# A row-sum kernel: the one-element copy ahead of the last VectorE operation becomes a waiting no-op, and SyncE's wait for ScalarE gets a no-op of its own

## The chip, the cores and the metric

One core of one Trainium2 chip; the experiments were spread over three chips, each beside the kernel before. The metric is device time in microseconds (us) of one execution. The profiler records one execution of each kernel; its span is some 1.8 us shorter than the device time. Nanoseconds (ns) below are the trace's own marks.

## The reference

```python
def setup_inputs():
    return {"x": np.random.randn(32, 512, 1024).astype(np.float32)}

def reference(x):
    return np.sum(x, axis=-1).astype(np.float32)
```

16,384 rows of 1,024 fp32 numbers are each summed: 67 MB in, 64 KB out.

## The kernel before

Rows go over the 128 partitions in two blocks of 112 and 16 rows a partition, 16 rows to a load. VectorE sums nearly all of them behind the loads. ScalarE helps towards the end. The change lies in the last block's last rows:

```python
CUT = 544
...
    part = rpool.tile([P, 1], F32, name="part")
    seen = rpool.tile([P, 1], F32, name="seen")
...
    def pairs_dve(xt, a, b, first, acc, pairs):
        h = (a + b) // 2
        nc.vector.tensor_tensor_reduce(
            out=pairs[:, 0 : h - a], in0=xt[:, a:h], in1=xt[:, h:b], scale=1.0, scalar=first,
            op0=ADD, op1=ADD, accum_out=acc,
        )
...
    cuts = [0, 9, 13, 15]            # loads of rows 0-8, 9-12, 13-14 ...
    last = 15 * D
    for i, k in ((0, CUT), (CUT, D)):    # ... and row 15 in two pieces
        nc.sync.dma_start(out=xt[:, last + i : last + k], in_=...)
...
    pairs_dve(xt, 13 * D, 14 * D, 0.0, res[:, c + 13 : c + 14], pairs[2])
    rows_act(xt, res, 14, 1, c + 14)
    pairs_dve(xt, last, last + CUT, 0.0, part, pairs[0])
    nc.vector.tensor_copy(out=seen, in_=part)
    pairs_dve(xt, last + CUT, last + D, part, res[:, c + 15 : c + 16], pairs[1])
    nc.sync.dma_start(out=out_b, in_=res)
```

One such operation adds the columns in pairs and sums the results, from `first` on. In the trace it is two instructions on the engine, the operation and a read of the accumulator (441 and 84 ns for row 15's first piece). Row 15's first piece leaves its sum in `part` (the *carried sum*), and the second piece starts from there. The copy to `seen` is of no use as a copy: it waits for `part` on a semaphore (a counter; the trace has it counted up at 157.703 us, 12 ns after the accumulator read's end, and the copy starts 23 ns later), and the operation behind it starts after the copy does: 99 ns after it.

Of the kernel before, what the change touches and what calls it, by code (L numbers as in the profile page):

```python
# [1 line left out]

# [4 lines left out]

F32 = mybir.dt.float32
ADD = mybir.AluOpType.add
COPY = mybir.ActivationFunctionType.Copy  # L10
X = mybir.AxisListType.X

BLOCKS = (112, 16)
G = 16
ACT_ROWS = 7
CUT = 544
EARLY = 2


@with_exitstack  # L20
def row_sums(
    ctx: ExitStack,
    tc: tile.TileContext,
    x: bass.AP,
    out: bass.AP,
):
    nc = tc.nc
    P = nc.NUM_PARTITIONS

    x_flat = x.flatten_outer_dims()  # L30
    R, D = x_flat.shape
    C = R // P
    assert R % P == 0 and sum(BLOCKS) == C
    out_flat = out.rearrange("a (b c) -> (a b c)", c=1)

    xpool = ctx.enter_context(tc.tile_pool(name="x", bufs=3))
    rpool = ctx.enter_context(tc.tile_pool(name="res", bufs=1))
    part = rpool.tile([P, 1], F32, name="part")
    seen = rpool.tile([P, 1], F32, name="seen")
    pairs = [rpool.tile([P, D // 2], F32, name=f"pairs{i}") for i in range(3)]  # L40

    def rows_dve(xt, res, j, n, c):
        nc.vector.tensor_reduce(  # L43
            out=res[:, c : c + n],
            in_=xt[:, j * D : (j + n) * D].rearrange("p (j d) -> p j d", d=D),
            axis=X,
            op=ADD,
        )

    def sum_act(v, acc):  # L50
        nc.scalar.activation(out=v, in_=v, func=COPY, accum_out=acc)  # L51

    def rows_act(xt, res, j, n, c):
        for i in range(n):
            sum_act(xt[:, (j + i) * D : (j + i + 1) * D], res[:, c + i : c + i + 1])

    def pairs_dve(xt, a, b, first, acc, pairs):
        h = (a + b) // 2
        nc.vector.tensor_tensor_reduce(  # L59
            out=pairs[:, 0 : h - a], in0=xt[:, a:h], in1=xt[:, h:b], scale=1.0, scalar=first,  # L60
            op0=ADD, op1=ADD, accum_out=acc,
        )

    def block(r0, n):
        x_b = x_flat[r0 : r0 + P * n].rearrange("(p c) d -> p (c d)", p=P)
        out_b = out_flat[r0 : r0 + P * n].rearrange("(p c) -> p c", p=P)
        return x_b, out_b, rpool.tile([P, n], F32, name=f"res{r0}")

    full = C - G
    done = 0  # L70
    for b, n in enumerate(BLOCKS):
        x_b, out_b, res = block(done * P, n)
        final = b == len(BLOCKS) - 1
        whole = n - G if final else n
        c = 0
        while c < whole:
            m = min(G, whole - c)
            xt = xpool.tile([P, G * D], F32, tag="xt", name="xt")
            parts = (0, 1, m) if done + c == 0 else (0, m)
            for i, k in zip(parts, parts[1:]):  # L80
                nc.sync.dma_start(
                    out=xt[:, i * D : k * D], in_=x_b[:, (c + i) * D : (c + k) * D]
                )
            a = ACT_ROWS if done + c + m == full else 0
            rows_dve(xt, res, 0, m - a, c)
            rows_act(xt, res, m - a, a, c + m - a)
            c += m
        if not final:

            for i, k in ((0, 104), (104, P)):  # L90
                nc.scalar.dma_start(out=out_b[i:k], in_=res[i:k])
        done += n

    xt = xpool.tile([P, G * D], F32, tag="xt", name="xt")
    cuts = [0, 9, 13, 15]
    for i, k in zip(cuts, cuts[1:]):
        nc.sync.dma_start(out=xt[:, i * D : k * D], in_=x_b[:, (c + i) * D : (c + k) * D])  # L97
    last = 15 * D
    for i, k in ((0, CUT), (CUT, D)):
        nc.sync.dma_start(  # L100
            out=xt[:, last + i : last + k],
            in_=x_b[:, c * D + last + i : c * D + last + k],
        )

    for i, k in zip(cuts[:2], cuts[1:3]):
        h = (k - i) // 2
        rows_dve(xt, res, i, h, c + i)
        rows_act(xt, res, i + h, k - i - h, c + i + h)
    pairs_dve(xt, 13 * D, 14 * D, 0.0, res[:, c + 13 : c + 14], pairs[2])
    rows_act(xt, res, 14, 1, c + 14)  # L110
    pairs_dve(xt, last, last + CUT, 0.0, part, pairs[0])


    nc.vector.tensor_copy(out=seen, in_=part)  # L114
    pairs_dve(xt, last + CUT, last + D, part, res[:, c + 15 : c + 16], pairs[1])
    nc.sync.dma_start(out=out_b, in_=res)


def kernel(tc: tile.TileContext, x: bass.AP, out: bass.AP):
    row_sums(tc, x, out)  # L120
    tc.close()
    tc.compile()  # L122



    sp = mybir.EngineType.SP
    fn = tc.nc.m.functions[0]
    entry, body = None, None
    for blk in fn.blocks:
        ops = [i for i in blk.instructions if i.engine == sp]  # L130
        if entry is None:
            entry = blk
        elif any(i.opcode == "DMACopy" for i in ops):
            body = blk
            break
    code = list(body.instructions)
    loads = [i for i in code if i.engine == sp][:EARLY]
    for load in loads:
        assert load.opcode == "DMACopy" and not load.sync_info.on_wait
        code.remove(load)  # L140
    body.instructions = code
    code = list(entry.instructions)
    at = next(k for k, i in enumerate(code) if i.engine == sp and i.opcode == "Drain")
    code[at:at] = loads
    entry.instructions = code

# [1 line left out]
_INS = ['x']  # L148
_OUTS = [((32, 512), 'float32')]


# [23 lines left out]
```

## Time and profile before

| | |
|---|---|
| device time, median of 6 runs beside the changed kernel (of 3 at the time of the prediction: 162.18 us) | 162.02 us (161.98 to 162.34) |
| span of the profiled run | 160.6 us |
| loads and their queue | 97.2% of the 16 engines' span |
| VectorE busy | 121.4 us, 76% |
| last piece's arrival to the store's issue | 563 ns |
| end of the first accumulator read to the store's issue | 673 ns |

The first rows say that the stream of loads sets the time; the last two are the stretch that the change can touch. The lines of that stretch stand in the prediction. One more view, the chain of waits followed back from the end, is worth having (start and duration in us; "issue" is time for which the profile shows no reason):

```profile
157.68 0.02 DVE part L59
157.70 0.02 issue
157.73 0.15 DVE seen L114
157.88 0.41 DVE pairs L59
```

It makes the copy (`seen`) a link of 0.15 us. It can't show that the last operation had begun at 157.82, before that link's end.

### The profile page before, as it was taken

What the parts mean: (1) busy time and instruction counts of PE and PEld (TensorE: products, weight loads), DVE (VectorE), ACT (ScalarE), POOL (GpSimd) and SP (SyncE); (2) the same over time, 40 slices, a digit from 0 to 9 for tenths busy, and PEclk for the clock granted to TensorE, in tenths of its full rate; (3) what the DMA queues carried; (4) which work ended last, traced back from release to release, by engine and by line L of the source; (5) the groups of instructions that cost most, each with busy time, mean ns of one, the idle gap of its engine ahead of it and who ended that gap; (6) DMA issues with size and microseconds to landing.
All of it is one profiled execution on the core that took longest, in us unless ns stands there. A gap on an engine that the chain in (4) does not pass through costs nothing.

```text
span 160.6 us, 120 instructions
## 1 busy us (share of the span) xinstructions
DVE 121.4 (76%) x16; ACT 17.2 (11%) x31; POOL 0.2 (0%) x4
## 2 busy tenths in 40 slices
DVE  0000059997799958999499994999949999598884
ACT  0000000000000000000000000000000000596892
POOL 0000000000000000000000000000000000000000
DMA  9997996996996996996996979979969969998991
GB/s 375 490 398 337 490 522 294 490 522 261 522 506 278 522 506 278 522 506 278 522 506 278 522 326 457 522 310 473 522 294 490 522 261 522 432 432 369 410 402 62
DMA packets 2169, 67.18 MB, mean 418 GB/s; under 512 B 505, under 2 KB 633, under 8 KB 889
## 3 DMA queue, kind: packets, MB, share of 16 engines
q1 hardware_dynamic: 2016, 67.12, 97.2%
q10 hardware_dynamic: 153, 0.06, 0.1%
HBM read 67.11 MB, written 0.07 MB: 418 GB/s over the span
## 4 chain that ended last, share of the span: by engine, by line
DMA 75%; DVE 22%; SPq 0%; issue 0%; DVEq 0%
DMA xt<-in_x_dram 75%; DVE res L43 21%; DVE pairs L59 1%; SPq L97 0%; DVE seen L114 0%; DVE part L59 0%; DVEq L122 0%; DVE res L59 0%
## 5 line engine op out<-in xcount | busy, mean ns | idle before, releaser
L43 DVE TENSOR_REDUCE res<-xt 128x16 f32<-128x16384 f32 (+3 forms) x9 | 119.8, 13309 | 36.6 <-DMA xt<-in_x_dram 36.6
L51 ACT ACT_TABLE_LOAD x1 | 1.3, 1283 | 138.3 <-DMA xt<-in_x_dram 138.3
L51 ACT ACTIVATE xt<-xt 128x1024 f32<-128x1024 f32 x15 | 15.6, 1042 | 2.2 <-DMA xt<-in_x_dram 2.2
L51 ACT ACTIVATION_READ_ACCUMULATOR xt<-xt 128x1 f32 x15 | 2.8, 186 | 0.0
L59 DVE CUSTOM_DVE_ANT_0 pairs<-xt 128x512 f32<-128x512 f32 (+1 forms) x2 | 1.1, 566 | 0.3 <-DMA xt<-in_x_dram 0.3
L59 DVE CUSTOM_DVE_ANT_0 pairs<-xt,part 128x240 f32<-128x240 f32 x1 | 0.5, 467 | 0.0
L114 DVE COPY seen<-part 128x1 f32<-128x1 f32 x1 | 0.2, 153 | 0.0
L59 DVE DVE_READ_ACCUMULATOR2_ANT res<- 128x1 f32 x2 | 0.2, 81 | 0.0
L159 POOL MEMSET const-bfloat16-1.0<- 128x1 bf16 x1 | 0.1, 101 | 0.0
L159 POOL MEMSET const-uint8-127<- 128x1 uint8 x1 | 0.1, 101 | 0.0
L159 POOL MEMSET const-float32-0.0<- 128x1 f32 x1 | 0.1, 98 | 0.2 <-issue 0.2
L159 POOL MEMSET const-float32-1.0<- 128x1 f32 x1 | 0.1, 98 | 0.0
L59 DVE DVE_READ_ACCUMULATOR2_ANT part<- 128x1 f32 x1 | 0.1, 84 | 0.0
## 6 DMA issues: line engine op xcount, KB each, us to landing
xt<-in_x_dram SPq DMA_DIRECT2D x1, 7680.0 KB
xt<-in_x_dram SPq DMA_DIRECT2D x1, 4608.0 KB, 32.4
xt<-in_x_dram SPq DMA_DIRECT2D x1, 2048.0 KB, 36.9
xt<-in_x_dram SPq DMA_DIRECT2D x1, 1024.0 KB, 39.0
xt<-in_x_dram SPq DMA_DIRECT2D x1, 512.0 KB, 3.9
xt<-in_x_dram SPq DMA_DIRECT2D x1, 272.0 KB, 39.1
xt<-in_x_dram SPq DMA_DIRECT2D x1, 240.0 KB, 38.9
xt<-in_x_dram SPq DMA_DIRECT2D x6, 40.9
```

Of the source, the lines that this page charges most:

```text
L43: nc.vector.tensor_reduce(out=res[:, c : c + n], in_=xt[:, j * D : (j + n) * D].rearrange("p (j d) -> p j d", d=D), axis=X, op=ADD,)
L51: nc.scalar.activation(out=v, in_=v, func=COPY, accum_out=acc)
L59: nc.vector.tensor_tensor_reduce(out=pairs[:, 0 : h - a], in0=xt[:, a:h], in1=xt[:, h:b], scale=1.0, scalar=first, op0=ADD, op1=ADD, accum ...
L114: nc.vector.tensor_copy(out=seen, in_=part)
L159: nc = _bacc.Bacc("TRN2", target_bir_lowering=False, num_devices=1)
```

## The change

The intent: take the copy's time off the end by waiting in an instruction that does nothing else, and let the last store wait for VectorE directly.

```diff
-CUT = 544
+CUT = 576
...
-    pairs_dve(xt, last, last + CUT, 0.0, part, pairs[0])
-    nc.vector.tensor_copy(out=seen, in_=part)
-    pairs_dve(xt, last + CUT, last + D, part, res[:, c + 15 : c + 16], pairs[1])
-    nc.sync.dma_start(out=out_b, in_=res)
+    carry = pairs_dve(xt, last, last + CUT, 0.0, part, pairs[0])
+    tc.keep_in_program_order(nc.vector.keepalive_nop([nc.vector.lower_ap(part)]))
+    total = pairs_dve(xt, last + CUT, last + D, part, res[:, c + 15 : c + 16], pairs[1])
+    tc.declare_no_dep(total.ins, carry.ins, reason="the wait is in the nop before it")
+    tc.keep_in_program_order(nc.sync.keepalive_nop([nc.sync.lower_ap(res[:, c + 14 : c + 15])]))
+    store = nc.sync.dma_start(out=out_b, in_=res)
+    for i in by_act:
+        tc.declare_no_dep(store.ins, i.ins, reason="the wait is in the nop before it")
```

(The tile `seen` goes, and the helpers return their instructions; `by_act` holds ScalarE's of the last block.) `keepalive_nop` is the no-op: it waits until the named tile is written and, in the trace, counts up a semaphore of its own when the wait is over (VectorE's no-op after the change: the carried sum's semaphore comes at 157.425 us, the no-op lasts from 157.452 to 157.473). `declare_no_dep` keeps the scheduler from adding a wait of its own.

More of the change, by code (lines that the diff above doesn't have):

```diff
@@ L38, in row_sums @@
     part = rpool.tile([P, 1], F32, name="part")
-    seen = rpool.tile([P, 1], F32, name="seen")
     pairs = [rpool.tile([P, D // 2], F32, name=f"pairs{i}") for i in range(3)]
@@ L50, in sum_act @@
     def sum_act(v, acc):
-        nc.scalar.activation(out=v, in_=v, func=COPY, accum_out=acc)
+        return nc.scalar.activation(out=v, in_=v, func=COPY, accum_out=acc)
+    by_act = []
     def rows_act(xt, res, j, n, c):
         for i in range(n):
-            sum_act(xt[:, (j + i) * D : (j + i + 1) * D], res[:, c + i : c + i + 1])
+            by_act.append(
+                sum_act(xt[:, (j + i) * D : (j + i + 1) * D], res[:, c + i : c + i + 1])
+            )
     def pairs_dve(xt, a, b, first, acc, pairs):
         h = (a + b) // 2
-        nc.vector.tensor_tensor_reduce(
+        return nc.vector.tensor_tensor_reduce(
             out=pairs[:, 0 : h - a], in0=xt[:, a:h], in1=xt[:, h:b], scale=1.0, scalar=first,
@@ L103, in row_sums @@
         )
+    by_act.clear()
     for i, k in zip(cuts[:2], cuts[1:3]):
```

## The prediction

> **What bounds the kernel now.** I read the page's split of the ending chain first, to see what the 160.6 us span is made of.
>
> ```profile
> DMA 75%; DVE 22%; SPq 0%; issue 0%; DVEq 0%
> HBM read 67.11 MB, written 0.07 MB: 418 GB/s over the span
> ```
>
> The kernel streams 67.11 MB and is bound by that stream nearly everywhere: 67.11 MB / 418 GB/s = 160.6 us. VectorE's 22% of the chain are reductions after which a load buffer comes free. The change touches nothing in there: it alters only what VectorE and SyncE do for the last row of the last block. So the whole question lies after about 156.6 us, and I read the timeline there: start, duration (both us), engine, line, operation, idle time before it.
>
> ```profile
> 156.62 0.69 DVE L59 CUSTOM_DVE_ANT_0 pairs<-xt 128x512 f32<-128x512 f32 x1 [0.26 <-DMA xt<-in_x_dram]
> 157.24 0.08 DVE L59 DVE_READ_ACCUMULATOR2_ANT res<- 128x1 f32 x1
> 157.24 0.44 DVE L59 CUSTOM_DVE_ANT_0 pairs<-xt 128x272 f32<-128x272 f32 x1
> 157.61 0.08 DVE L59 DVE_READ_ACCUMULATOR2_ANT part<- 128x1 f32 x1
> 157.73 0.15 DVE L114 COPY seen<-part 128x1 f32<-128x1 f32 x1
> 157.82 0.47 DVE L59 CUSTOM_DVE_ANT_0 pairs<-xt,part 128x240 f32<-128x240 f32 x1
> 158.22 0.08 DVE L59 DVE_READ_ACCUMULATOR2_ANT res<- 128x1 f32 x1
> 158.36 0.35 SPq L116 DMA_DIRECT2D out_dram<-res  x1
> ```
>
> The copy to be removed is the fifth line. The next operation starts at 157.82, before the copy's end at 157.88. It seems to be released by the copy, and the chain of waits counts the copy as a link. But the last 480 columns also have to be there. The issues of the last two loads and the time from issue to landing say when:
>
> ```profile
> 118.12 0.44 SPq L100 DMA_DIRECT2D xt<-in_x_dram  x1
> 118.91 0.33 SPq L100 DMA_DIRECT2D xt<-in_x_dram  x1
> DMA to landing us min/median/max: 38.9/39.0/39.1
> ```
>
> 118.12 + 39.1 = 157.22 for the first piece (544 columns) and 118.91 + 38.9 = 157.81 for the second. (To the nanosecond the trace's arrivals are 157.217 and 157.801; the last operation starts at 157.825, 24 ns after its data.) That 24 ns is what every operation here needs when data release it: row 13's load lands at 156.601 and the operation starts at 156.625. So **the last operation is released by its data, with the copy at most level with it.** This is the reading on which the prediction rests.
>
> [...] Directly released: 24 ns from landing to start, as above. Behind a wait of its own there is one case on VectorE, at the first reduction, whose data are complete at 21.977 us by the trace's arrivals:
>
> ```profile
> L43 DVEq EVENT_SEMAPHORE  x1: 21/21/21, 22.0 to 22.0; - x1
> 22.08 17.22 DVE L43 TENSOR_REDUCE res<-xt 128x16 f32<-128x16384 f32 x1 [22.08 <-DMA xt<-in_x_dram]
> ```
>
> 22.076 - 21.977 = 99 ns instead of 24 ns. [...] The trace has the sizes: from 272 to 512 columns the time grows by 692 - 441 = 251 ns, 1.046 ns a column, so 157 ns of either is fixed, and the copy's 153 ns is nothing else. The one with the carried scalar is 467 - 251 = 216: 59 ns more than the rule. Either it waits inside for the copy (0.41 us from the copy's end to its own end is just 251 + 157), or fetching a scalar from SBUF costs that much.
>
> **The change, part by part.**
>
> *CUT 544 to 576.* The pairs go from 272 and 240 to 288 and 224 columns. No byte more is moved, so the last landing stays at 157.80. The first piece is 32 columns x 4 B x 128 = 16 KB longer and lands 16 KB / 418 GB/s = 39 ns later, at 157.256; its operation starts at about 157.280 instead of 157.243 and takes 458 instead of 441 ns, so the carried sum is there (with its accumulator read, 7 ns behind the operation's end, and 12 ns for the semaphore) at about 157.757 instead of 157.703. The last operation is 16 columns, 17 ns, shorter.
>
> *The copy goes, a wait comes.* By the 99 ns above, the last operation can start at 157.757 + 0.099 = 157.856. Its data let it start at 157.825. So the wait ends last, and the start moves **31 ns later** although a 153 ns instruction is gone. The duration is 467 - 17 = 450 if the scalar fetch is what costs 59 ns, 391 if the copy did it. End: 158.306 or 158.247, against 158.292 before: **+14 or -45 ns**. I give two chances in three to the fetch, since the 272-column operation likewise began before its forerunner's end (157.243 against 157.317) and paid nothing for it: 14 x 2/3 - 45 x 1/3 = -6 ns.
>
> *SyncE's wait for ScalarE moves ahead.* In the kernel before, the built program has the wait on VectorE's result in an instruction of its own, and the store behind it carries the wait on ScalarE, long fulfilled. The accumulator read ends at 158.300, that wait ends at 138.27 + 20.07 = 158.33, the store is issued at 158.364: 64 ns.
>
> ```profile
> L116 SPq EVENT_SEMAPHORE  x1: 20068/20068/20068, 138.3 to 138.3; - x1
> ```
>
> In the changed program the no-op takes ScalarE's wait and the store carries VectorE's itself. How fast that is shows at a load that waits on a reduction in just that way:
>
> ```profile
> 99.55 17.22 DVE L43 TENSOR_REDUCE res<-xt 128x16 f32<-128x16384 f32 x1 [2.24 <-DMA xt<-in_x_dram]
> 116.80 1.28 SPq L97 DMA_DIRECT2D xt<-in_x_dram  x3
> ```
>
> The reduction ends at 116.767 and the load is issued at 116.795: 28 ns. So **36 ns are saved**, all on the path. ScalarE's last column is there at 157.78, some 0.5 us before VectorE's, so the no-op is out of the way by then.
>
> *The rest.* From the store's issue to its landing takes 1.4 us, and 0.8 us of closing waits follow; I expect neither to move. The sum is -6 - 36 = about -42 ns, from 162.18 to **162.14 us**: 0.03%.
>
> **The rivals.** First, the face value of the chain of waits: the copy goes with its 153 ns and its link costs little, so 0.10 to 0.15 us are gained on VectorE and 162.0 us come out. For it speaks that the copy is a link of that chain; against it the landing at 157.801, before which nothing can start: from the old start, at most the 59 ns within the operation and 17 ns of columns can be won there, 0.11 us with SyncE's part. Second, the no-op is dearer on VectorE than I think[...], and then the start slips beyond 157.86. A further 0.1 us would eat the gain and make it 162.24. Third, something far from the edit moves: a packet size (2,304 and 1,792 B per partition instead of 2,176 and 1,920), the place of a tile after one was dropped, or the last landing. Both pieces together are 512 KB of 67 MB, and the loads' order and waits are unchanged, so this should be under 0.05 us either way. Fourth, the edit could be hidden completely, with 162.18 again; it would need the store's wait not to be on the path, which the timeline contradicts.
>
> **Range and chances.** All these outcomes lie within 0.15 us of before. What decides the measured number is the scatter between runs: the three runs before go from 162.02 to 162.34 us, four times the effect. I take 161.90 to 162.36. For over 2% either way 3.2 us would have to change, more than all that comes after the last landing (160.6 - 157.8 = 2.8 us)[...], so 1% on either side is enough.
>
> **What would show each step.** In the changed kernel's profile the copy's line should be gone, with 119 instructions; the 224-column operation should start at 157.83 to 157.88 on the same landing, some 0.1 us after the accumulator read ends, instead of at once behind the copy; its duration should be 0.45 us (fetch) or 0.39 us (copy). The store should come 28 ns after the last accumulator read ends, not 64. Shifted to the same last landing, the store's issue should be 0.02 to 0.1 us earlier. The prediction is wrong if the last operation starts well before 24 ns after its landing, if the wait on VectorE costs more than 0.2 us, or if the landing of the last load moves by 0.1 us or more.

No term of the sum is among them; it came to -6 - 36 = about -42 ns. That the 99 ns of the first reduction hold for the no-op too was my estimate from that one case. The 24 ns are what both traces have, before and after: every VectorE operation that waits for a load starts 22 to 26 ns after the arrival, but for the first reduction (99 and 98) and the one behind the no-op (132).

## The result

162.13 us, median of 6 runs (162.10 to 162.54), against 162.02 of the kernel before in the same rounds: ratio 1.0007, 95% interval 0.9994 to 1.002. (All ratios here are the mean time of one kernel's fast runs over that of the other's of the same rounds, so not quite the ratio of the medians quoted.) The clock can't tell the two apart. The trace can. VectorE's timeline of the changed kernel, with the store's issue:

```profile
156.31 0.69 DVE L62 CUSTOM_DVE_ANT_0 pairs<-xt 128x512 f32<-128x512 f32 x1 [0.35 <-DMA xt<-in_x_dram]
156.93 0.08 DVE L62 DVE_READ_ACCUMULATOR2_ANT res<- 128x1 f32 x1
156.95 0.46 DVE L62 CUSTOM_DVE_ANT_0 pairs<-xt 128x288 f32<-128x288 f32 x1
157.33 0.08 DVE L62 DVE_READ_ACCUMULATOR2_ANT part<- 128x1 f32 x1
157.60 0.45 DVE L62 CUSTOM_DVE_ANT_0 pairs<-xt,part 128x224 f32<-128x224 f32 x1 [0.19 <-DMA xt<-in_x_dram]
157.98 0.08 DVE L62 DVE_READ_ACCUMULATOR2_ANT res<- 128x1 f32 x1
158.09 0.35 SPq L124 DMA_DIRECT2D out_dram<-res  x1
```

Where before VectorE stood still for only 35 ns between the last two sums (from the carried sum's read to the copy), there is now a hole of 0.19 us ahead of the last one. The page puts it down to the load. That is a trap of this view: by the arrivals of this trace the last piece was there at 157.468, 132 ns before the start. The chain of waits has it right:

```profile
157.41 0.02 DVE part L62
157.43 0.03 issue
157.45 0.02 DVEq L118
157.47 0.13 issue
157.60 0.45 DVE pairs L62
```

L118 is the no-op. It takes 0.02 us, and behind it come 0.13 us in which nothing is waited for that the profile knows of. In the copy's place the end now has a hole that is longer than the copy was (0.15 us). On SyncE, the queue's waits (in all, times, longest; us) show the other half of the change, which did what it should. Before:

```profile
SPq L116 <- DVE res L59: 39.1, 1, 39.1
```

After:

```profile
SPq L123 <- ACT xt L50: 38.6, 1, 38.6
SPq L124 <- DVE res L62: 0.5, 1, 0.5
```

The no-op (L123) takes ScalarE's wait, and the store (L124) waits for VectorE by itself: it is issued 29 ns after the last accumulator read ends, where it was 64.

Counted from the last piece's arrival, so that the time of that arrival drops out, the store is issued after 621 ns instead of 563: **58 ns later**, of which the last operation's start is +108 (132 - 24), its length -16 (451 - 467), the accumulator read's tail +1 and the store's wait -35. What follows the issue is unchanged (1,411 ns to its landing, 1,415 before). This sets one trace of each kernel against the other; the control below shows how far it holds for other traces.

### The profile page after: what moved, and what is told of

Its sections match the earlier page's. It is cut to its first block, busy times and chain, and to the rows that moved or that the text cites. A ratio compares the mean times of both kernels' runs of the same rounds, so it can differ in the third digit from the quotient of the medians.

```text
span 160.3 us, 121 instructions
## 1 busy us (share of the span) xinstructions
DVE 121.3 (76%) x15; ACT 17.2 (11%) x31; POOL 0.2 (0%) x4
## 4 chain that ended last, share of the span: by engine, by line
DMA 75%; DVE 22%; SPq 0%; issue 0%; DVEq 0%
DMA xt<-in_x_dram 75%; DVE res L42 21%; DVE pairs L62 1%; SPq L100 0%; DVEq L118 0%; DVE part L62 0%; DVEq L132 0%; DVE res L62 0%
## 5 line engine op out<-in xcount | busy, mean ns | idle before, releaser
L62 DVE CUSTOM_DVE_ANT_0 pairs<-xt,part 128x224 f32<-128x224 f32 x1 | 0.5, 451 | 0.2 <-DMA xt<-in_x_dram 0.2
```

What stands on the lines that cost most here:

```text
L62: return nc.vector.tensor_tensor_reduce(out=pairs[:, 0 : h - a], in0=xt[:, a:h], in1=xt[:, h:b], scale=1.0, scalar=first, op0=ADD, op1=ADD ...
```

## The experiments

Theory: behind a waiting no-op the next operation starts late (127 ns after the wait's end in the trace after), while behind the copy it starts before the copy's end (157.825 against 157.879 us before); this costs more than the copy. Rivals: the shifted cut did it; the scalar from SBUF; the second wait, on the load.

### The cut alone

```diff
-CUT = 544
+CUT = 576
```

> Only the cut moves (544 to 576 columns); copy and SyncE's combined wait stay. Yardstick in each trace: from the last load's arrival to the start of the last VectorE operation (24 ns before, 132 ns after the change) and to the store's issue (563 before, 621 after). Theory: the carried sum now comes 43 ns ahead of the last arrival instead of 98, the copy is then the later of the two releases, the operation starts 55 to 80 ns after the arrival, is 16 ns shorter, and the store is issued at 580 to 605 ns: the cut alone costs 15 to 40 ns. Rival (the copy never binds): start at 24 ns, store at 547, the cut alone wins 16 ns. Time within 0.1% of before either way.

Measured: start 58 ns after the last arrival, 442 ns long, store at 573: 10 ns later than before, so the copy did become the later release, 106 ns after the first accumulator read's end. The operation was 9 ns shorter than after the change (442 against 451), with the copy still running at its start; that I had not expected, and it makes the cost 10 instead of 15 or more. By the clock 162.16 against 162.17 us, ratio 1.0002 (0.9989 to 1.0014). The cut does not explain 58 ns.

### VectorE's no-op alone

```diff
-    nc.vector.tensor_copy(out=seen, in_=part)
+    tc.keep_in_program_order(nc.vector.keepalive_nop([nc.vector.lower_ap(part)]))
```

(Cut: `declare_no_dep` between the two sums, as in the change.)

> Only the copy gives way to VectorE's no-op; cut 544 and SyncE's combined wait stay. Theory (the no-op costs some 175 ns from the carried sum's semaphore to the start of the operation behind it[...]): start about 77 ns after the last arrival instead of 24, duration 467, store issued at about 616 ns after it instead of 563. Rival (the 127 ns after the no-op in the changed kernel came from the shifted cut, not the no-op): start at 24 to 30 ns, store at 563.

Measured: start 144, length 468, store at 683. The 187 ns from the end of the accumulator read to the start are the same as after the change, with the cut at 544: the no-op brings the hole, the cut does not. The start missed my 77 since the carried sum was ready 43 ns before the last arrival instead of 110, which I had taken over from the trace before. The two pieces were only 18 ns closer together (566 instead of 584); the rest is that the first piece landed 562 instead of 616 ns behind row 13's load, so that its operation waited for row 13's and started 79 ns after its data. By the clock 162.22 us, ratio 1.0007 (0.9993 to 1.0021).

### SyncE's no-op alone

```diff
+    tc.keep_in_program_order(nc.sync.keepalive_nop([nc.sync.lower_ap(res[:, c + 14 : c + 15])]))
-    nc.sync.dma_start(out=out_b, in_=res)
+    store = nc.sync.dma_start(out=out_b, in_=res)
+    ...  # declare_no_dep on ScalarE's instructions, as in the change
```

> Only SyncE's wait on ScalarE moves into a no-op of its own; copy and cut 544 stay. Theory: last operation as before (24 ns after the arrival, 467 ns), the store follows the accumulator read's end by 28 ns instead of 64, so it is issued 527 ns after the last arrival instead of 563. Rival (the combined wait cost nothing and the 29 ns of the changed kernel are chance): 563. If the theory holds, this part alone is the better kernel, by 36 ns of 162 us, which the clock can hardly tell.

Measured: start 25, store 27 ns after the accumulator read and 529 ns after the arrival. The part gains what was foreseen, in the trace. The clock says 162.20 us, ratio 1.0004 (0.9991 to 1.0017), and so nothing.

### The waits by themselves, 12 links each

After the result is out of VectorE's hands, chains of this kind run (cut; the others have the copy in the no-op's place, no wait but the operation's own, an immediate instead of the scalar, or a plain reduction):

```diff
+    for i in range(12):
+        keep(nc.vector.keepalive_nop([nc.vector.lower_ap(ma[i])]))
+        two = keep(pairs_dve(xt, 0, 64, ma[i], ma[i + 1], junk[1]))   # scalar: the sum before
```

> The disputed waits by themselves: after the result, chains of 12 links on 64 columns (32 pairs), each link needing the carried sum of the one before. From the end of the accumulator read to the start of the next operation. Theory[...]: with no-op about 185 ns, also without a scalar from SBUF; a plain reduction behind a no-op 60 to 110 ns; with the copy 110 to 130; where the operation carries the wait itself 35 ns. Rival A (the scalar's fetch makes it long): the no-op without a scalar from SBUF is at 60 to 110 like the reduction. Rival B (the second wait, on the load, made it long): all no-op chains at 60 to 110. The scalar from SBUF should add 59 ns to the duration of an operation in every chain that has one, and to the period of operations without waits if it holds the engine (rival: hidden).

The groups by shape (line, engine, operation, names, shapes and count, then busy us and mean ns, then the idle time ahead of them):

```profile
L59 DVE CUSTOM_DVE_ANT_0 jself<-xt,na 128x32 f32<-128x32 f32 x12 | 3.0, 252 | 0.4
L59 DVE CUSTOM_DVE_ANT_0 jnop<-xt,ma 128x32 f32<-128x32 f32 x12 | 3.0, 252 | 2.5 <-DVE ma L59 2.5
L59 DVE CUSTOM_DVE_ANT_0 jcopy<-xt,la 128x32 f32<-128x32 f32 x12 | 2.9, 242 | 0.0
L59 DVE CUSTOM_DVE_ANT_0 jimm<-xt 128x32 f32<-128x32 f32 x13 | 2.5, 193 | 2.2 <-DVE oa L59 2.2
L169 DVE TENSOR_REDUCE ra<-xt 128x1 f32<-128x32 f32 x12 | 2.2, 187 | 1.8
```

(`jself` is the chain with the operation's own wait, `jimm` the one with a no-op and no scalar, `ra` the reductions behind a no-op.) With the no-op 2.5 us of idle time stand before 12 operations, with the copy none (0.4 before the copies), with the operation's own wait 0.4. From the trace's marks of a regular link, in ns:

| chain | accumulator read's end to the operation's start | of it after the no-op's end | a link |
|---|---|---|---|
| own wait | 36 | | 296 |
| copy | 106 | | 356 |
| no-op | 188 | 128 | 448 |
| no-op, no scalar from SBUF | 187 | 127 | 387 |
| no-op, plain reduction | 146 (from the reduction's end) | 86 | 333 |

So rival A falls (the hole is there without a scalar), and rival B too (no load is waited for). The hole is only partly the custom operation's: a reduction behind the same no-op starts after 86 ns, above the 49 ns that I had read off the first reduction of the kernel. My 60 to 110 for the reduction, counted from the end before, was too low: 146. The copy, at 105 to 106, lies just under my 110 to 130. The scalar from SBUF costs 59 ns in length (252 against 193), as predicted. Whether it holds the engine was to be shown by chains without waits, but these had waits after all (0.4 us of idle time before 12 operations, as with the own wait), since each operation overwrote the one before's output; that test is void. With the same waits, behind a no-op, a link was 61 ns longer with the scalar (448 against 387).

### Neither copy nor no-op

```diff
-    nc.vector.tensor_copy(out=seen, in_=part)
```

> Copy taken out of the kernel before and nothing put in its place; the scheduler then makes the two waits of the last operation itself: one instruction that waits for the last landing and updates no semaphore, and the wait for the carried sum in the operation. Theory:[...] the operation starts 90 to 130 ns after that wait ends, some 140 to 180 ns after the last arrival instead of 24, and the store is issued 680 to 715 ns after it. Within that, 128 ns as in the chains would say that the no-op's own semaphore update costs nothing, 90 that it costs some 37 ns. Rival (only a no-op with an update of its own is dear): start at 50 to 80 ns.

Measured: the scheduler's own wait ends 49 ns after the arrival, the operation starts 85 ns behind it, at 134, and the store is issued at 675, each 5 or 6 ns under the range I had given.

```profile
157.32 0.02 DVEq L58
157.34 0.09 issue
157.42 0.47 DVE pairs L58
```

Behind a wait that updates no semaphore of its own there is a hole too, so this rival falls; but the distance is 85 instead of 128 ns. Together with the first reduction of the kernel there are four combinations, each the distance from the wait's end to the next start:

| | plain reduction | custom operation |
|---|---|---|
| wait without update | 49 (one place; 49 to 50 in all 14 traces) | 85 (one case) |
| no-op with an update of its own | 86 | 128 |

About 36 to 42 ns go with the custom operation and 37 to 43 with the no-op's update. The update was not varied by itself, so its share rests on this table alone. 161.98 us in its single run is no verdict.

### The chains by the clock, 100 links

The same chains alone, of 100 links, with the copy, with the no-op and with the operation's own wait:

```diff
-        keep(nc.vector.tensor_copy(out=lb[i], in_=la[i]))          # with the copy
+        keep(nc.vector.keepalive_nop([nc.vector.lower_ap(la[i])]))    # with the no-op; neither: own wait
```

> The chain with the copy, 100 links behind the result, for the clock instead of the trace. From the 12-link chain: 356 ns a link, so the kernel should end about 35.7 us after the first link's start, near 162.2 - 2.3 + 36 = 196 us in all. Theory and rival differ in the comparison with the next two runs.

> The same with the no-op in the copy's place: 448 ns a link by the trace, so 92 ns x 100 = 9.2 us slower than the chain with the copy. Rival (the trace's start and end marks mislead and the two cost the same, or the no-op less, by the clock): within 1 us of it or faster.

> The same with neither copy nor no-op: the operation waits for the carried sum itself. 296 ns a link by the trace, 6.0 us faster than the chain with the copy, 15.2 us faster than that with the no-op.

Medians of 4 runs each: 196.43 us with the copy, 206.29 with the no-op, 190.49 with the operation's own wait. So by the clock the no-op costs (206.29 - 196.43) / 100 = 99 ns a link more than the copy, and the own wait 59 ns less. The trace's 92 and 60 are confirmed; the 7 ns more come from three of the 100 no-op links that took 654 to 809 ns instead of 447, which neither other chain has (at most 358); one of the 12 above took 655. They were not held up at one place: two lost the time before the no-op, one before the accumulator read, one behind the no-op. What held them up stays open.

### A version meant to beat both

Copy and cut as before, SyncE's no-op as after, and the carried sum as one more column instead of a scalar:

```diff
+    rest = D - CUT
+    tail = rpool.tile([P, rest + 2], F32, name="tail")     # last piece, carried sum, a zero
+    part = tail[:, rest : rest + 1]
+    nc.vector.memset(tail[:, rest + 1 : rest + 2], 0.0)
-    pairs_dve(xt, last + CUT, last + D, part, res[:, c + 15 : c + 16], pairs[1])
+    pairs_dve(tail, 0, rest + 2, 0.0, res[:, c + 15 : c + 16], pairs[1])
```

(The last piece's load now goes to `tail`.)

> A version meant to beat both: copy and cut 544 as before, SyncE's no-op as after, and the carried sum no longer a scalar operand: it is written beside the last 480 columns (with a zero), so the last operation reads 241 pairs and an immediate. Theory: copy or landing release it as before (24 ns after the last arrival, or 71 ns after the copy's start if that is later), it takes 157 + 252 = 409 ns instead of 467, the store follows the accumulator read by 28 instead of 64: 24 + 409 + 8 + 28 = about 470 ns after the last arrival instead of 563, if the arrival releases it. Rival (the 59 ns were not the scalar's fetch): 467 stays and the store is at 528. The time should fall by 0.09 us, 0.06%, too little for the clock.

```profile
157.58 0.15 DVE L122 COPY seen<-tail 128x1 f32<-128x1 f32 x1
157.67 0.41 DVE L66 CUSTOM_DVE_ANT_0 pairs<-tail 128x241 f32<-128x241 f32 x1
```

Measured: start 24, length 411, store at 470 ns after the arrival, 93 ns earlier than before and 151 earlier than after. That is the best end of all traces, and its clock is 162.02 against 161.99 us, ratio 0.9999 (0.9985 to 1.0013): not shown to be faster.

### The changed kernel again, and the kernel before against itself

Neither kernel was edited.

> The changed kernel once more, for its trace and its time on another chip. Theory: from the carried sum's semaphore to the last operation's start 175 ns, its duration 451, store 29 ns after the accumulator read; time 0 to 0.1% above before, not told apart from before by the clock. The interval to the last arrival may differ by some tens of ns, since the arrivals do.

> The kernel before, unchanged, timed against itself: what the clock's comparison gives where nothing differs, and a second trace of it. Theory (a shift of 0.1% between two kernels of one job can be the arrival of the 67 MB stream rather than the edit): the ratio lies within 0.999 to 1.001 of 1, its interval some 0.1% wide on either side; last arrival in the trace anywhere from 157.2 to 157.9 us; the store is issued 530 to 610 ns after it, 63 ns after the accumulator read. Rival (the clock is good to 0.03%): ratio within 0.9997 to 1.0003.

> The changed kernel a third time, beside the control. From the traces the edit alone costs 0.05 us where the carried sum or the arrival binds as before, at most 0.1 us: ratio 1.0003 to 1.0006 within a scatter of 0.001. If it is again at 1.0016 while the control is at 1.000, something in addition to the traced 0.05 us differs, and the trace should show where: a later last arrival.

The changed kernel came to 162.23 against 161.99 us (ratio 1.0016, 1.0004 to 1.0029) and, on another chip, to 162.29 against 162.25 (0.9999, 0.9985 to 1.0013). The kernel before, against itself, came to 162.20 against 162.25 (0.9995, 0.9982 to 1.0009). The traces of the changed kernel repeat within 10 ns. So the 0.24 us of the one comparison are four times what the edit does in the trace, and a repetition did not have them. Where they came from was not found; that trace, of the run with 162.11 us, has its last arrival no later (157.462) than the first one's.

The control's trace corrected my reading of the kernel before. Its last landings came closer together (row 13's load, the first piece and the last at 156.463, 156.974 and 157.546: 1,083 ns in all instead of 1,200). The first piece's operation therefore waited for row 13's, which it follows by 618 ns, and not for its data; the carried sum was late, and there the copy released the last operation:

```profile
156.49 0.69 DVE L59 CUSTOM_DVE_ANT_0 pairs<-xt 128x512 f32<-128x512 f32 x1 [0.35 <-DMA xt<-in_x_dram]
157.10 0.08 DVE L59 DVE_READ_ACCUMULATOR2_ANT res<- 128x1 f32 x1
157.10 0.44 DVE L59 CUSTOM_DVE_ANT_0 pairs<-xt 128x272 f32<-128x272 f32 x1
157.47 0.08 DVE L59 DVE_READ_ACCUMULATOR2_ANT part<- 128x1 f32 x1
157.59 0.15 DVE L114 COPY seen<-part 128x1 f32<-128x1 f32 x1
157.66 0.46 DVE L59 CUSTOM_DVE_ANT_0 pairs<-xt,part 128x240 f32<-128x240 f32 x1
```

The operation starts 71 ns after the copy, as in every chain link, and 110 ns after the arrival, and is 458 instead of 467 ns long. The store, at 640, is outside the 530 to 610 that I had expected. The traces of the kernels with rounds, in ns from the last piece's arrival (without the 100-link chains):

| kernel | carried sum read | last op starts | its length | read's end to store | store issued |
|---|---|---|---|---|---|
| before | -110 | 24 | 467 | 64 | 563 |
| before, control | 4 | 110 | 458 | 64 | 640 |
| cut alone | -48 | 58 | 442 | 65 | 573 |
| SyncE's no-op alone | -91 | 25 | 469 | 27 | 529 |
| sum as a column | -103 | 24 | 411 | 29 | 470 |
| after | -55 | 132 | 451 | 29 | 621 |
| after, again | -50 | 136 | 451 | 28 | 624 |
| after, third | -58 | 129 | 451 | 27 | 615 |
| VectorE's no-op alone | -43 | 144 | 468 | 63 | 683 |

With the copy the start is the later of arrival + 24 and carried sum + 106; with the no-op it is carried sum + 187 in every row. The rows fit within 1 ns.

The four traces of the chains, whose links run after an unchanged ending, add to the rows of the kernel before: carried sum read at -26, 32, 22 and 63, start at 80, 137, 127 and 169, store at 610, 666, 656 and 701 (12 links; 100 links with the copy, the no-op and the own wait). They keep the rule within 1 ns. So in five of six traces of the unchanged ending the copy binds, and the one that the prediction was read from is the exception. Its 563 ns is the earliest store of the six, and the 58 ns hold against it alone. What decides is how soon the first piece lands behind row 13's load: after 616 ns in that trace, 443 to 530 in the five. With the cut at 576 it was 624 to 757 ns in four traces, with 544 it was 443 to 671 in ten; whether the longer piece or the scatter of the stream does that, no run was made to show.

Set against the control, the changed kernel's store looks early, but there the carried sum was late. From the carried sum's read to the store it takes 636 ns in the control and 676 after, and the cut adds 17 ns of columns ahead of it: 57 ns more. By this estimate, which leaves out that the longer piece lands later, the change costs where the copy binds about what it does where the arrival binds.

## Why the prediction was right, and where it was wrong

- **The time**: 162.14 us foretold, 162.13 measured, within 2%. This tests little: the range came from the scatter between runs, and the agreement to 0.01 us is luck. The kernel before came to 162.18 us at the time and to 162.02 in the rounds of the result, so the foretold change of -0.04 us came out as +0.11, which the clock can't tell from nothing. (The scatter that is called "four times the effect" is nearly eight times: 0.32 against 0.042 us.)
- **The last bytes release the last operation**: right for the trace it was read from, and the reason why the copy's 153 ns were not to be gained there. As a general reading it was too narrow: in the other five traces of that ending the copy binds.
- **"By the 99 ns above, the last operation can start at 157.757 + 0.099 = 157.856"**: this step failed. The carried sum's semaphore came at 157.425 in the trace after, and the operation started at 157.600: 175 ns, not 99. I had taken the figure from a wait that updates nothing, in front of a plain reduction; here a no-op with an update of its own stands in front of a custom operation, and the four combinations above give 37 to 43 ns for the one and 36 to 42 for the other, together about the missing 76. The prediction's second rival had named a start beyond 157.86 for a dearer no-op. So the start moved by 108 ns instead of 31. That is 77 of the 100 ns between the sum foretold (-42) and the one in the trace (+58); 20 more come from weighing in the branch that did not come true (-6 where the other branch alone has +14). The sign of the small effect was wrong. What goes on in the engine during the hole is not shown; the runs show its length alone: 186 to 188 ns from the accumulator read's end to the custom operation's start, in the regular links of the 12-link chains and in the four endings with the no-op.
- **The 59 ns belong to the scalar from SBUF**: right, 451 ns where 450 was foretold for that branch, and 252 against 193 ns in the chains. The smaller odds went to the copy, with which the operation is some 9 ns *shorter* where the copy releases it (458 against 467 in the control, 242 against 252 in the chains).
- **The store's wait, 36 ns**: right, 35 measured, and 27 to 29 ns in all five runs that have it.
- **The rest unchanged**: right (1,411 against 1,415 ns from issue to landing). The 39 ns by which the first piece was to land later can't be tested: it landed 638 ns after row 13's load instead of 616, but this distance scatters by more than 100 ns between traces of either cut.
- **119 instructions**: wrong. The page counts 121; it counts waiting instructions, so the copy's loss is outweighed by two no-ops.

## What to carry to other kernels

That an instruction only waits did not make it free here. A 153 ns copy, whose successor overlaps half of it, was the cheaper wait: the operation behind it started 106 ns after the carried sum instead of 187, and a link of the chain was shorter by 92 ns in the trace and 99 by the clock. Let the operation carry the wait that ends last itself, as the store does after the change (27 to 29 ns behind the accumulator read instead of 63 to 65) and the chain with its own wait did (36 ns instead of 106 or 188), and put a wait into a separate instruction only where it is over early enough. On SyncE ScalarE's was, by some 0.5 us. On VectorE the no-op had the earlier wait too, and still lost: the carried sum came 50 to 58 ns before the last arrival, and by the rule above it would have had to come some 163 ns before it (187 - 24, an estimate). A scalar from SBUF cost 59 ns an operation here (252 against 193 ns on 32 pairs), and handing the value over as one more column saved it (411 ns for 241 pairs against 467 for 240). And before counting a removed link as a gain, look up when the other input of the next operation arrives, in more than one trace.
